# Seven of eight feed-forward layers read their tokens in another order, on one Trainium2 core

## The chip, the cores and the metric

The program runs on one core of one Trainium2 chip. The metric is the device time of one execution in microseconds, from the core's first instruction to its last with what lies around it. The median of the two timed runs of the kernel before is 2019.77 us, and both runs gave that same number.

## The reference: what is computed

An encoder of 4 blocks works on 256 tokens of width 1024. Each block adds to the residual stream a half-weighted SwiGLU feed-forward layer, then a mixer, then another half-weighted feed-forward layer; each part starts with an RMS norm. The mixers are a gated short convolution (blocks 0 and 3), a Hyena long convolution (block 1) and a gated delta rule (block 2). A last RMS norm ends it. The part that matters here is the feed-forward layer, eight times:

```
def swiglu(x, w_in, w_out):            # D = 1024, D_FF = 2816
    g, u = jnp.split(x @ w_in, 2, axis=-1)
    return (jax.nn.silu(g) * u) @ w_out

x = x + 0.5 * swiglu(rms_norm(x, norms[i, 0]), ffn_w_in[i, 0], ffn_w_out[i, 0])
```

All numbers are float32, and each product is computed to nearly that precision.

## The kernel before, in words

**Layout.** Activations are held transposed: features on the 128 partitions, the 256 tokens along each partition. A tile of the residual stream `x` is 128 x 512, two blocks of 128 features side by side, each with 256 tokens.

**Products.** Every operand of a large product is split into a high and a low part of type float32r (`wh`, `wl` for the weights; `xh`, `xl` for the normed input; `hh`, `hl` for the gated hidden values). The helper `mm3` (lines 325 to 329) then issues three matmuls into the same PSUM area: high times high (L327), low weight times high (L328), high weight times low (L329). In each, a 128 x 128 block of weights is the stationary operand, loaded by its own weight-load instruction, and 128 x 256 of tokens is the moving operand that streams through, one column for each token. The product is accumulated into 256 float32 columns of PSUM, half a bank.

**A feed-forward layer** (`ffn`, line 465). For each of 22 blocks of 128 hidden features, `proj` (line 302) forms gate and up parts over the 8 blocks of input features, into the two halves of the PSUM tile `g`: 2 x 8 calls of `mm3`. VectorE and ScalarE scale, apply SiLU, multiply and split the result (`gate`, line 471, and `split`, line 452). Two blocks later `acc_pair` (line 400) multiplies that hidden block by its row block of `w_out` into eight output areas, the halves of the four PSUM tiles `accf`: 8 calls of `mm3`. So a layer has 22 x 24 x 3 = 1584 matmuls and as many weight loads. Near the start of each layer a few small matmuls in plain float32 sum the squares (`pst`, L373) and spread the norm factor (`pbc`, L383). `finish` (line 412) adds the four accumulators to `x` and prepares the next layer's operands tile by tile.

**The order of the work.** The order of each engine's instructions is that in which the program text issues them. Weights come in 1 MB transfers on SyncE's queue into a ring of 2 buffers, ScalarE (L282) and VectorE (L284) split them into rings of 5 buffers, and TensorE uses one pair for 24 matmuls. Waits between engines come from the tiles' readers and writers. In layer 0 the preparation of the Hyena filters runs between the products, among it three-matmul products with 512 columns (`sp`).

**Numbering.** The 12 parts are numbered 0 to 11 (`norm_index`): feed-forward layers are 0, 2, 3, 5, 6, 8, 9 and 11; the mixers are 1 (short convolution), 4 (Hyena), 7 (delta rule) and 10 (short convolution). `run` (line 1483) goes through them.

Of the kernel before, what the change touches and what calls it, by code (L numbers as in the profile page):

```python
# [20 lines left out]
L = 256  # L21
# [25 lines left out]
def norm_index(ph):  # L47
    if ph[0] == "ffn":
        return ph[1] * 3 + 2 * ph[2]
    return ph[1] * 3 + 1  # L50
# [70 lines left out]
class Cols:  # L121
    def __init__(self):
        self.n = 0
        self.at = {}
# [90 lines left out]

class Prog:
    def __init__(self, nc, tc, io, phases, pools):
        self.nc, self.tc, self.io, self.phases = nc, tc, io, phases  # L220
# [103 lines left out]

    def mm3(self, out, ah, al, bh, bl, start, stop):
        mm = self.nc.tensor.matmul
        mm(out, ah, bh, start=start, stop=False, skip_group_check=True)  # L327
        mm(out, al, bh, start=False, stop=False, skip_group_check=True)  # L328
        mm(out, ah, bl, start=False, stop=stop, skip_group_check=True)  # L329
# [1153 lines left out]
    def run(self):  # L1483
        tc = self.tc
        self.setup()
        self.start()
        ph = self.phases
        ng = norm_index(ph[0])
        self.split_x(0, ng)
        self.ready.append(self.cut_part())  # L1490
        for m in range(1, 4):
            self.split_x(m, ng)
        self.ready.append(self.cut_part())
        self.ready.append(self.cut_part())
        for m in range(4):
            self.square_x(m, ng)
        kinds = [p[0] for p in ph]
        hyp = fip = None
        if "hy" in kinds:
            hyp = tc.tile_pool(name="hp", bufs=1)  # L1500
            self.hp = hyp.__enter__()
            fip = tc.tile_pool(name="fp", bufs=1)
            self.fp = fip.__enter__()
            self.hy_setup()
        self.setup_rest()
        for n, p in enumerate(ph):
            nxt = norm_index(ph[n + 1]) if n + 1 < len(ph) else None
            ng = norm_index(p)
            if nxt is None:
                tqp = tc.tile_pool(name="tq", bufs=1)  # L1510
                self.tq = tqp.__enter__()
                self.final_setup()
            if p[0] == "ffn":
                self.ffn(ng, nxt)
            elif p[0] == "sc":
                self.sc(ng, p[2], nxt)
            elif p[0] == "hy":
                self.drain_bg()
                fip.__exit__(None, None, None)
                with tc.tile_pool(name="tq", bufs=1) as self.tq:  # L1520
                    self.hy(ng, nxt)
                hyp.__exit__(None, None, None)
            else:
                with tc.tile_pool(name="gq", bufs=1) as self.gq:
                    self.gd(ng, nxt)
        self.final()
        tqp.__exit__(None, None, None)
# [49 lines left out]
```

## Time and profile before

| What | Value |
|---|---|
| Median of two runs | 2019.77 us (both the same) |
| The profiled execution's own time | 2015.31 us |
| Its span, first to last instruction | 2013.4 us |
| Mean granted TensorE clock | 0.993 |
| Matmuls, and weight loads | 17234 each |
| TensorE matmul busy (modelled ends) | 99% of the span |
| VectorE, ScalarE busy | 70%, 50% |
| HBM traffic | 353.11 MB read, 176 GB/s |

How to read it: PE is TensorE's matmul side and PEld its weight-load side, which overlap. Matmuls are pipelined, so the duration printed for one matmul is longer than the time from its start to the next one's start. It is that second number, the pace, that adds up to the span; it comes from counting matmuls in a stretch or from the starts in the timeline.

### The profile page before, as it was taken

The numbers are of one execution on the slowest core, as the hardware profiler recorded it, in microseconds if no ns is written. First come the engines' busy times: TensorE is split into PE (matmuls) and PEld (weight loads), VectorE is DVE, ScalarE is ACT, GpSimd is POOL, SyncE is SP. The second block draws the span as 40 slices with busy tenths as digits, with TensorE's granted clock in tenths as the row PEclk, the third lists the DMA queues.
The fourth block names the chain that finished last, engine by engine and source line by source line (L and its number), as shares of the span: only waits on it lengthen the run. The fifth ranks groups of instructions, "written<-read, shape, count | busy, mean of one in ns | idle before, by whom it ended". The sixth has DMA issues, their size and how long they took to land.

```text
span 2013.4 us, 40294 instructions
## 1 busy us (share of the span) xinstructions
PE 1986.9 (99%) x17234; PEld 1966.1 (98%) x17234; DVE 1405.1 (70%) x2155; ACT 1015.0 (50%) x1546; POOL 74.0 (4%) x75
## 2 busy tenths in 40 slices
PE   9999999999999999999999999899999999999998
PEld 9999999999999999999999988789999999999998
DVE  6765867666766798666766689957667666777664
ACT  6444545445544555444544467545445544545443
POOL 0000000000000120000000012000000000000000
PEclk9999999999999999999999999899999999999999
DMA  7644445555555533555555633304654655565552
GB/s 246 233 167 167 168 168 186 184 184 180 196 201 191 178 142 123 208 188 189 184 193 191 208 126 126 127 23 174 205 197 167 218 192 191 186 209 176 201 193 101
DMA packets 93989, 356.76 MB, mean 177 GB/s; under 512 B 5809, under 2 KB 7217, under 8 KB 93618
## 3 DMA queue, kind: packets, MB, share of 16 engines
q1 hardware_dynamic: 93666, 354.18, 50.7%
q8 instruction: 135, 2.21, 0.4%
q14 instruction: 44, 0.36, 0.1%
q10 hardware_dynamic: 144, 0.00, 0.0%
HBM read 353.11 MB, written 1.05 MB: 176 GB/s over the span
## 4 chain that ended last, share of the span: by engine, by line
PE 87%; DVE 7%; DMA 2%; ACT 2%; issue 1%; POOL 0%; SPq 0%; POOLq 0%; DVEq 0%; ACTq 0%
PE g L329 16%; PE g L328 16%; PE g L327 16%; PE accf L329 8%; PE accf L328 8%; PE accf L327 8%; DVE wl L284 2%; DMA raw<-w 2%; PE c L328 1%; PE c L327 1%; PE c L329 1%; PE accs L328 1%; PE b L328 1%; PE accs L327 1%; PE b L327 1%
## 5 line engine op out<-in xcount | busy, mean ns | idle before, releaser
L284 DVE TENSOR_TENSOR wl<-raw,wh 128x1024 fp32r<-128x1024 f32 (+1 forms) x667 | 810.8, 1221 | 396.6 <-ACT wh L282 396.1
L282 ACT ACTIVATE wh<-raw 128x1024 fp32r<-128x1024 f32 (+1 forms) x667 | 695.8, 1052 | 604.9 <-PE g L329 401.9
L327 PE MATMUL g<-xh,wh 128*128 128x256 f32 x2816 | 783.7, 278 | 0.1
L329 PE MATMUL g<-xl,wh 128*128 128x256 f32 x2816 | 782.4, 278 | 0.0
L328 PE MATMUL g<-xh,wl 128*128 128x256 f32 x2816 | 782.2, 278 | 0.1
L327 PEld LDWEIGHTS g<-xh,wh 128*128 128x128 f32 x2816 | 529.3, 188 | 3.1 <-ACT wh L282 2.7
L328 PEld LDWEIGHTS g<-xh,wl 128*128 128x128 f32 x2816 | 529.8, 188 | 0.5 <-DVE wl L284 0.4
L329 PEld LDWEIGHTS g<-xl,wh 128*128 128x128 f32 x2816 | 529.2, 188 | 0.0
L329 PE MATMUL accf<-hl,wh 128*128 128x256 f32 x1408 | 390.8, 278 | 0.8 <-DVE hl L458 0.8
L327 PE MATMUL accf<-hh,wh 128*128 128x256 f32 x1408 | 390.4, 277 | 0.0
L328 PE MATMUL accf<-hh,wl 128*128 128x256 f32 x1408 | 390.4, 277 | 0.0
L327 PEld LDWEIGHTS accf<-hh,wh 128*128 128x128 f32 x1408 | 264.1, 188 | 1.2 <-ACT hh L457 0.8
L329 PEld LDWEIGHTS accf<-hl,wh 128*128 128x128 f32 x1408 | 264.2, 188 | 1.0 <-DVE hl L458 1.0
L328 PEld LDWEIGHTS accf<-hh,wl 128*128 128x128 f32 x1408 | 264.4, 188 | 0.1
L457 ACT ACTIVATE hh<-t 128x256 fp32r<-128x256 f32 x192 | 79.7, 415 | 195.3 <-DVE t L477 189.3
L458 DVE TENSOR_TENSOR hl<-t,hh 128x256 fp32r<-128x256 f32 x192 | 81.3, 424 | 69.6 <-ACT hh L457 69.6
L474 DVE TENSOR_TENSOR t<-g,rs 128x256 f32<-128x256 f32 x176 | 74.4, 423 | 63.5 <-PE g L329 56.9
L475 ACT ACTIVATE t<-t 128x256 f32<-128x256 f32 x176 | 71.0, 404 | 27.0 <-DVE t L474 26.8
L328 PE MATMUL p<-xh,wl 128*128 128x256 f32 x256 | 73.5, 288 | 8.8 <-DVE wl L284 8.8
L327 PE MATMUL p<-xh,wh 128*128 128x256 f32 x256 | 74.8, 292 | 2.0 <-ACT wh L282 2.0
L477 DVE TENSOR_TENSOR t<-t,t 128x256 f32<-128x256 f32 x176 | 73.6, 418 | 1.6 <-ACT t L475 1.4
L329 PE MATMUL p<-xl,wh 128*128 128x256 f32 x256 | 73.2, 286 | 0.0
(315 smaller groups left out, 2407.0 us busy)
## 6 DMA issues: line engine op xcount, KB each, us to landing
raw<-w SPq DMA_DIRECT2D x330, 1024.0 KB, 4.7
raw<-w SPq DMA_DIRECT2D x6, 256.0 KB, 5.4
x<-x SPq DMA_DIRECT2D x4, 256.0 KB, 4.4
raw<-w SPq DMA_DIRECT2D x2, 512.0 KB, 6.3
dec<-dec SPq DMA_DIRECT2D x1, 1024.0 KB, 7.2
traw<-dft SPq DMA_DIRECT2D x2, 512.0 KB, 6.3
out<-ob SPq DMA_DIRECT2D x4, 256.0 KB, 2.4
w<-w SPq DMA_DIRECT2D x1, 512.0 KB, 9.1
```

The source lines that it names most:

```text
L282: nc.scalar.activation(hi[:, s], src[:, s], AF.Copy)
L284: nc.vector.tensor_tensor(lo[:, s], src[:, s], hi[:, s].bitcast(F32), op=ALU.subtract)
L327: mm(out, ah, bh, start=start, stop=False, skip_group_check=True)
L328: mm(out, al, bh, start=False, stop=False, skip_group_check=True)
L329: mm(out, ah, bl, start=False, stop=stop, skip_group_check=True)
L457: self.nc.scalar.activation(hh, src, AF.Copy)
L458: self.nc.vector.tensor_tensor(hl, src, hh.bitcast(F32), op=ALU.subtract)
L474: nc.vector.tensor_tensor(t1, pg[f][:, :L], self.rs, op=ALU.mult)
L475: nc.scalar.activation(t1, t1, AF.Silu)
L477: nc.vector.tensor_tensor(t2, t1, t2, op=ALU.mult)
```

## The change

A table gives seven of the eight feed-forward layers an order for the 256 tokens, and `mm3` applies it to the two moving operands and to the output area alike, where the moving operand has 256 columns. The k-th column that streams in is another token than before, and its result goes to that token's place in PSUM, so that PSUM holds the same values at the same places. The stationary operands, the number of matmuls, all other engines' instructions and all transfers are as before. Layer 11 and the mixers have no entry and keep the plain order.

```
+ORDERS = {
+    0: ("p (a b c) -> p b a c", 2, 16),
+    2: ("p (b a c) -> p a b c", 2, 16),
+    3: ("p (b a c) -> p a b c", 4, 16),
+    5: ("p (a b c) -> p b a c", 2, 8),
+    6: ("p (a b c) -> p b a c", 2, 4),
+    8: ("p (a b c) -> p b a c", 4, 16),
+    9: ("p (a b c) -> p b a c", 2, 32),
+}
+
+def ordered(ap, ng):
+    if ng not in ORDERS:
+        return ap
+    how, a, c = ORDERS[ng]
+    return ap.rearrange(how, a=a, c=c)
...
     def mm3(self, out, ah, al, bh, bl, start, stop):
         mm = self.nc.tensor.matmul
+        if bh.shape[1] == L:
+            out, bh, bl = (ordered(t, self.layer) for t in (out, bh, bl))
         mm(out, ah, bh, start=start, stop=False, skip_group_check=True)
         mm(out, al, bh, start=False, stop=False, skip_group_check=True)
         mm(out, ah, bl, start=False, stop=stop, skip_group_check=True)
...
-            ng = norm_index(p)
+            self.layer = ng = norm_index(p)
```

In words, with the tokens cut into runs of c neighbours (a float32 has 4 bytes):

| Layer | Order of the runs | Run | Runs in 256 |
|---|---|---|---|
| 0 | one of the first half, one of the second half, in turn | 16 tokens, 64 bytes | 16 |
| 2 | all even-numbered runs, then all odd-numbered | 16, 64 bytes | 16 |
| 3 | every fourth run, in four passes | 16, 64 bytes | 16 |
| 5 | first half, second half, in turn | 8, 32 bytes | 32 |
| 6 | first half, second half, in turn | 4, 16 bytes | 64 |
| 8 | the four quarters in turn | 16, 64 bytes | 16 |
| 9 | first half, second half, in turn | 32, 128 bytes | 8 |

## Rows read from the trace of the kernel before

**Rows 1.** The profile page: its head line and TensorE's busy time.

```profile
span 2013.4 us, 40294 instructions
...
PE 1986.9 (99%) x17234; PEld 1966.1 (98%) x17234; DVE 1405.1 (70%) x2155; ACT 1015.0 (50%) x1546; POOL 74.0 (4%) x75
```

**Rows 2.** The page's chain of work that ended last, shares by engine.

```profile
PE 87%; DVE 7%; DMA 2%; ACT 2%; issue 1%; POOL 0%; SPq 0%; POOLq 0%; DVEq 0%; ACTq 0%
```

**Rows 3.** Groups by shape on TensorE: count, busy us, mean ns, idle before.

```profile
L327 PE MATMUL g<-xh,wh 128*128 128x256 f32 x2816 | 783.7, 278 | 0.1
...
L327 PE MATMUL accf<-hh,wh 128*128 128x256 f32 x1408 | 390.4, 277 | 0.0
```

**Rows 4.** Waits of TensorE, the longest in total: us, times, longest.

```profile
PE p L328 <- DVE wl L284: 8.8, 2, 5.8
```

**Rows 5.** Stretches of layers 2, 3, 5, 6, 8, 9, 11, 0: length; busy and count by engine.

```profile
330.00:490.00 160.00, 160.00 (x1361) 160.00 (x1360) 98.59 (x135) 71.63 (x95) 0.00 (x0) 1.00 0.56 191
520.00:680.00 160.00, 160.00 (x1414) 160.00 (x1413) 102.82 (x141) 76.07 (x103) 0.00 (x0) 1.00 0.58 197
810.00:980.00 170.00, 170.00 (x1446) 170.00 (x1445) 106.90 (x146) 77.70 (x103) 0.00 (x0) 1.00 0.53 187
1000.00:1160.00 160.00, 160.00 (x1414) 160.00 (x1414) 102.27 (x141) 74.43 (x99) 0.00 (x0) 1.00 0.58 198
1390.00:1550.00 160.00, 160.00 (x1414) 160.00 (x1414) 105.44 (x146) 76.58 (x103) 0.00 (x0) 1.00 0.60 205
1570.00:1730.00 160.00, 160.00 (x1414) 160.00 (x1413) 103.48 (x143) 75.92 (x102) 0.00 (x0) 1.00 0.59 203
1840.00:1990.00 150.00, 150.00 (x1326) 150.00 (x1326) 97.02 (x131) 71.03 (x94) 0.00 (x0) 1.00 0.56 194
...
72.00:112.00 40.00, 40.00 (x342) 40.00 (x341) 27.26 (x41) 20.07 (x26) 0.00 (x0) 1.00 0.65 218
```

**Rows 6.** Timeline of layer 3 around `pbc`: start us, duration us, instruction.

```profile
509.32 0.28 PE L328 MATMUL g<-xh,wl 128*128 128x256 f32 x1
...
510.15 0.28 PE L329 MATMUL g<-xl,wh 128*128 128x256 f32 x1
510.27 0.38 PE L383 MATMUL pbc<-msk,r 128*128 128x128 f32 x2
...
510.60 0.28 PE L328 MATMUL g<-xh,wl 128*128 128x256 f32 x1
...
511.51 0.28 PE L327 MATMUL g<-xh,wh 128*128 128x256 f32 x1
```

**Rows 7.** Timeline of layer 2 at its `pbc`.

```profile
322.99 0.43 PE L383 MATMUL pbc<-msk,r 128*128 128x128 f32 x2 [0.24 <-POOL r L377]
...
323.38 0.28 PE L328 MATMUL g<-xh,wl 128*128 128x256 f32 x1
...
323.73 0.28 PE L328 MATMUL g<-xh,wl 128*128 128x256 f32 x1
```

**Rows 8.** Timeline of layer 0: twelve float32r matmuls of 512 columns.

```profile
168.03 0.39 PE L327 MATMUL sp<-eoh,th 128*128 128x512 f32 x1
...
169.64 0.39 PE L328 MATMUL sp<-eoh,tl 128*128 128x512 f32 x1
...
170.55 0.40 PE L329 MATMUL sp<-eol,th 128*128 128x512 f32 x1
```

**Rows 9.** Timeline of layer 7: eight weight loads for narrow matmuls, then 512-column matmuls.

```profile
1183.85 0.98 PEld L927 LDWEIGHTS ew<-g,msk 128*128 128x128 f32 x8
...
1184.74 0.30 PEld L916 LDWEIGHTS dc<-B,msk 128*128 128x128 f32 x2
...
1185.71 0.38 PE L917 MATMUL dc<-outside,idb 128*128 128x512 bf16 x1
1185.93 1.02 PE L916 MATMUL dc<-B,msk 128*128 128x512 f32 x2
1186.79 0.38 PE L917 MATMUL dc<-outside,idb 128*128 128x512 bf16 x1
```

## The prediction, made before the change was run

> **What bounds the kernel now.** I read the page's head first [rows 1]: 17234 matmuls in 2013.4 us, 117 ns for each on average, and TensorE busy 99% of the time. Then the chain of waits [rows 2]: 87% of it is TensorE's own work, so the reader sees an engine that follows itself. Then the groups by shape [rows 3]: the three lines of `mm3` in `g` (3 x 2816) and in `accf` (3 x 1408) are 12672 matmuls, 1584 in each of eight layers, with next to no idle time before them. The longest sum of TensorE's waits is 8.8 us, and it is in a mixer [rows 4]. So the end is set by the pace of the 256-column matmuls, and the printed 278 ns says nothing on that; counts in a stretch do.
>
> **Two paces.** The stretches inside the layers [rows 5], length by count: layers 2 and 5 give 160/1361 and 170/1446, both 117.6 ns; layers 3, 6, 8, 9 and 11 give 160/1414 and 150/1326, 113.1 or 113.2 ns; layer 0 about 117 (40/342). The granted clock is 1.00 in all of them, so this is not the clock. Same instructions, same shapes, two paces, each kept for a whole layer. Layer 3 shows where the pace is chosen [rows 6]: 7 steps take 0.83 us before the `pbc` pair (118.6 ns), 8 steps take 0.91 us after it (113.8 ns). In layer 2 the same pair waits for the norm factor, and the three steps behind it take 0.35 us (117 ns) [rows 7]. A layer on the slower pace costs 1584 x 4.4 ns = 7.0 us. The profiled execution took 2015.31 us, 4.46 us under the median of 2019.77; that is two thirds of one such layer, so I take it as about the size by which one execution differs from another here.
>
> **What sets the pace.** A column needs 0.417 ns at the 2.4 GHz level that is granted, 256 columns 106.7 ns. The 113.2 ns are 6% over that. A weight load is 128 columns: eight loads in a row start 0.89 us before the next, 111.3 ns each [rows 9], which could be the bound. But matmuls of 512 columns have two load times to hide one load in, and they too take 229 ns on average over 11 steps, 227.5 over the last four, where 213.3 would do [rows 8]: again 6 to 7% over. A bf16 matmul of 512 columns takes 0.22 us [rows 9]. So I read the pace as that at which float32r columns come through, in a stream without slack, with the loads close behind at 111.3 ns.
>
> **The change, part by part.** No instruction, load, wait or transfer is added, removed or moved. SyncE's queue, VectorE's readers of PSUM (which read the same area in the plain order) and the counts on all engines stay; VectorE, busy 99 us of 160 in a layer's stretch [rows 5], has room if TensorE should run faster. What changes is the address pattern of 7 x 1584 = 11088 matmuls, at the input and at the output. In place of one run of 256 columns there are 16, 16, 16, 32, 64, 16 and 8 runs (layers 0, 2, 3, 5, 6, 8, 9): 168 in all, 161 breaks, times 1584 are 255,024 breaks. The one question is the price of a break.
>
> The trace of before has no float32r matmul with a broken pattern. The nearest row is the bf16 matmul of 512 columns that reads one run of 128 four times, three breaks: 0.22 us to the next start, against 213.3 ns for its columns [rows 9]. At 215.5 ns (eight of them took 0.21 to 0.22) its excess is 2.2 ns, so a break costs at most 0.73 ns even if all of it is theirs: the upper end, 255,024 x 0.73 ns = 186 us, 2201 us. The lower end is a gain: if another order of the addresses takes away what holds the stream back, the loads hold it at 111.3 ns: 3 x 1584 x 6.3 + 4 x 1584 x 1.9 = 29.9 + 12.0 = 42 us, 1973 us. I take zero for a break, since the row with breaks is within 1% of its columns' bare time; then only the paces are drawn anew, each layer at one of its two. All three slow layers turned fast would give 4752 x 4.4 = 21 us back, all four fast ones turned slow cost 6336 x 4.4 = 28 us: 1994 to 2043.
>
> The Trainium skill, "TensorE: Matmul & The Clock Gate", section "Back-to-back issue gap", gives N/2.4 + 2.5 ns between matmuls, 109 ns for 256 columns. The trace does not agree, it has 113 and 118; by the page 4 to 8 ns in each matmul would be slack in which breaks could hide, and the first rival below would come to an estimated 2065 us rather than 2122.
>
> **The rivals.**
>
> First, slower: each break costs one column's time, 0.417 ns, in the stream that sets the pace. For it: the float32r stream already runs 16 columns' time late in 256 (113.2 - 106.7 = 6.5 ns), which the bf16 row does not, so something in that path pauses and new addresses may add pauses; nothing hides them. Against it: the bf16 row. Price 255,024 x 0.417 = 106 us: 2122. By layer, in ns for each matmul: 6 in layers 0, 2, 3, 8, 13 in layer 5, 26 in layer 6, 3 in layer 9. It passes 2% from 0.16 ns a break on. Chance 0.22, its size open between 2060 and 2201.
>
> Second, the pauses that exist come once in 16 columns, that is once in 64 bytes, and a run shorter than that brings its own. 6.5 ns are 16 pauses of one column's time, so the number fits, but nothing in the rows shows where in a matmul they fall. Then only layers 5 (16 more) and 6 (48 more) pay: 64 x 0.417 x 1584 = 42 us, 2057. Layer 6 alone would go from 113 to 133 ns. Chance 0.13, about half of it on either side of 2%.
>
> Third, PSUM takes the broken output at half pace. The row for that is the plain float32 matmul, which spends 0.86 us on 512 columns in two passes [rows 9], so 215 ns at 256 columns in two: 11088 x 100 ns = 1.1 ms, about 3100 us. No row speaks for it, none excludes it. Chance 0.04. The Trainium skill, "Advanced Engine Details and Errata", section "PSUM Cachelines", says that any non-contiguous pattern significantly slows matmuls, and next to it that every two consecutive elements should be contiguous; the shortest run here has four, so by its second sentence nothing happens. No run here shows either yet.
>
> Fourth, faster: the other orders free the stream down to the load's pace, 1973 us. For it: two paces under one instruction stream say that something interferes, and that it depends on how two streams meet. Against it: it would have to work in nearly all seven layers at once. Chance 0.05.
>
> Fifth, the change does nothing: the patterns of input and output are permuted alike, so a lowering that sorts them makes the plain order of both. Then 2015 to 2020. Chance 0.03.
>
> **How the numbers follow.** The forecast, breaks for nothing, has 0.53. I put it at 2017 us, between the profiled 2015.3 and the median 2019.8, since the paces may fall either way. 2% of the median is 40 us, about what a measurement of this kernel can tell from no change. Within 2%: 0.53 + 0.03 + 0.07 of the second rival = 0.63. Slower: 0.22 + 0.06 + 0.04 = 0.32. Faster: 0.05. The range begins at 1990, just under the forecast's own low end (the faster case left out, 0.05), and ends at 2125, just over the first rival's price (half of that rival, 0.11, and the third, 0.04, left out): 0.20 outside.
>
> **What would show it.** Pace by layer, from counts in the same stretches. Right: seven layers at 113 or 118, layer 6 no worse than layer 9, layer 11 as before. First rival: excess in proportion to the breaks, 7 : 15 : 31 : 63 for layers 9, 0, 5, 6. Second: layers 0, 2, 3, 8, 9 unchanged, 5 and 6 slower. Third: all seven near 215. Fourth: paces under 113. The mixers' paces may shift by the 4.4 ns with the layer ahead of them. The forecast is wrong if any layer leaves the two paces, above all layer 6 with its 64 runs.

## The result and the profile after

The changed kernel takes 2080.76 us (2079.63 and 2081.88), the kernel before 2019.77: slower by 3.0%, ratio 1.0302 with a 95% interval of 1.0258 to 1.0346. The profiled execution took 2079.63 us, 64.3 us over the profiled one of before. The time lies inside the range that was given, well above the 2017 us that was forecast.

The head of the page after, its chain of waits by engine, one matmul group and the longest wait of TensorE, to set against [rows 1 to 4]:

```profile
span 2077.9 us, 40314 instructions
...
PE 2053.6 (99%) x17234; PEld 2032.5 (98%) x17234; DVE 1406.8 (68%) x2155; ACT 1016.8 (49%) x1546; POOL 73.9 (4%) x75
...
PE 92%; DVE 4%; ACT 1%; DMA 1%; issue 1%; POOL 0%; SPq 0%; POOLq 0%; DVEq 0%; ACTq 0%
...
L349 PE MATMUL g<-xh,wh 128*128 128x256 f32 x2816 | 800.2, 284 | 0.3 <-ACT wh L302 0.3
```

```profile
PE p L350 <- DVE wl L304: 7.6, 2, 4.6
```

The counts of busy instructions on all five engines are the same (the 20 more in the head are of kinds not counted as busy), the longest wait is no longer than before, and TensorE's share of the chain has grown. So the time went into the pace. Stretches inside layers 2, 3, 5, 6, 8, 9, 11 and 0 of the kernel after (length; busy and count of PE, PEld, VectorE, ScalarE, GpSimd; clock, DMA share, GB/s), to set against [rows 5]:

```profile
330.00:490.00 160.00, 160.00 (x1336) 160.00 (x1335) 98.23 (x135) 71.34 (x95) 0.00 (x0) 1.00 0.54 185
520.00:680.00 160.00, 160.00 (x1350) 160.00 (x1349) 99.08 (x137) 72.26 (x96) 0.00 (x0) 1.00 0.53 185
830.00:990.00 160.00, 160.00 (x1299) 160.00 (x1299) 94.49 (x128) 68.39 (x91) 0.00 (x0) 1.00 0.52 181
1020.00:1190.00 170.00, 170.00 (x1344) 170.00 (x1344) 99.13 (x136) 74.24 (x97) 0.00 (x0) 1.00 0.50 175
1430.00:1590.00 160.00, 160.00 (x1350) 160.00 (x1349) 101.28 (x139) 73.61 (x100) 0.00 (x0) 1.00 0.56 191
1620.00:1780.00 160.00, 160.00 (x1336) 160.00 (x1335) 97.66 (x133) 71.10 (x94) 0.00 (x0) 1.00 0.54 190
1900.00:2050.00 150.00, 150.00 (x1326) 150.00 (x1326) 100.16 (x140) 73.16 (x98) 0.00 (x0) 1.00 0.57 197
72.00:112.00 40.00, 40.00 (x336) 40.00 (x335) 27.10 (x40) 19.49 (x26) 0.00 (x0) 1.00 0.61 217
```

The reader divides length by count. (A count takes in two or three matmuls that are under way at the ends of the stretch, so each pace is low by about 0.2 ns, by about 0.6 in layer 0's short stretch; the differences hardly change.) Each layer has 1584 of these matmuls.

| Layer | Runs | ns before | ns after | us added |
|---|---|---|---|---|
| 0 | 16 of 64 bytes | 117.0 | 119.0 | 3.3 |
| 2 | 16 of 64 bytes | 117.6 | 119.8 | 3.5 |
| 3 | 16 of 64 bytes | 113.2 | 118.5 | 8.5 |
| 5 | 32 of 32 bytes | 117.6 | 123.2 | 8.9 |
| 6 | 64 of 16 bytes | 113.2 | 126.5 | 21.1 |
| 8 | 16 of 64 bytes | 113.2 | 118.5 | 8.5 |
| 9 | 8 of 128 bytes | 113.2 | 119.8 | 10.5 |
| 11 | plain | 113.1 | 113.1 | 0 |

The last column adds up to 64.3 us. That the two profiled executions differ by the same 64.3 us is in part chance, for something else moved too: the mixer between layers 9 and 11, whose products are plain in both kernels, fell from the faster plain pace to the slower. A stretch of it before, then after:

```profile
1750.00:1810.00 60.00, 60.00 (x532) 60.00 (x531) 45.52 (x69) 29.75 (x37) 0.00 (x0) 1.00 0.61 207
```

```profile
1810.00:1870.00 60.00, 60.00 (x511) 60.00 (x511) 43.66 (x67) 28.42 (x36) 0.00 (x0) 1.00 0.60 207
```

That is 112.8 and 117.4 ns. From the last matmul of layer 9 to the first of layer 11 it took 87.9 us before and 91.2 after, 3.3 us more. Read in the same way, from starts in the traces, the seven layers took 62.2 us longer and the delta rule's part 1.1 us less. So about 62 of the 64 us are the price of the new order.

### The profile page after: what moved, and what is told of

The parts are those of the page before. It is cut to its first block, busy times and chain, and to the rows that moved or that the text cites. A ratio compares the mean times of both kernels' runs of the same rounds, so it can differ in the third digit from the quotient of the medians.

```text
span 2077.9 us, 40314 instructions
## 1 busy us (share of the span) xinstructions
PE 2053.6 (99%) x17234; PEld 2032.5 (98%) x17234; DVE 1406.8 (68%) x2155; ACT 1016.8 (49%) x1546; POOL 73.9 (4%) x75
## 4 chain that ended last, share of the span: by engine, by line
PE 92%; DVE 4%; ACT 1%; DMA 1%; issue 1%; POOL 0%; SPq 0%; POOLq 0%; DVEq 0%; ACTq 0%
PE g L349 16%; PE g L350 16%; PE g L351 16%; PE accf L349 8%; PE accf L351 8%; PE accf L350 8%; PE c L350 1%; PE c L351 1%; PE c L349 1%; DVE wl L304 1%; DMA raw<-w 1%; PE accs L350 1%; PE xv L351 1%; PE accs L351 1%; PE b L350 1%; PE b L351 1%
## 5 line engine op out<-in xcount | busy, mean ns | idle before, releaser
L349 PE MATMUL g<-xh,wh 128*128 128x256 f32 x2816 | 800.2, 284 | 0.3 <-ACT wh L302 0.3
L350 PE MATMUL g<-xh,wl 128*128 128x256 f32 x2816 | 798.7, 284 | 0.8 <-DVE wl L304 0.8
L351 PE MATMUL g<-xl,wh 128*128 128x256 f32 x2816 | 798.7, 284 | 0.0
L349 PE MATMUL accf<-hh,wh 128*128 128x256 f32 x1408 | 399.4, 284 | 0.0
L351 PE MATMUL accf<-hl,wh 128*128 128x256 f32 x1408 | 399.3, 284 | 0.0
L350 PE MATMUL accf<-hh,wl 128*128 128x256 f32 x1408 | 399.1, 283 | 0.0
```

## The experiments

Theories at the start: A, the read of the moving operand pays; B, the write into PSUM pays; C, the stream and the weight loads get in each other's way. Each is told apart by pace and not by total alone, because each layer can carry an order of its own. All rows are of the view just shown. Where no number of runs is given, a total is of one execution.

### Input or output

Only the moving operands are reordered in the first kernel, only the output in the second, so in both the products land on other tokens' places:

```
-            out, bh, bl = (ordered(t, self.layer) for t in (out, bh, bl))
+            bh, bl = (ordered(t, self.layer) for t in (bh, bl))     # in_only
+            out = ordered(out, self.layer)                          # out_only
```

> The new orders at the moving operand alone; the output goes to PSUM in the plain order, so the products of seven layers land on other tokens' places. Theory A, the read of the moving operand in SBUF is what pays: paces as with the whole change, 120 ns in layers 0, 2 and 9, 118.8 in 3 and 8, 123.4 in 5, 126.7 in 6, about 2080 us. Theory B, the write into PSUM pays: all layers at 113 or 118 ns, 2010 to 2030 us. Both pay: paces between, 2030 to 2065 us.

> The mirror image: the new orders at the output alone, the moving operand read in plain order (again the results land on other tokens' places). Theory A (read): 113 or 118 ns in every layer, 2010 to 2030 us. Theory B (write): the paces of the whole change, about 2080 us, with layer 6 at 127 ns.

The input alone took 2082.48 us, the output alone 2020.65, beside 2018.34 for the kernel before. Layers 6 and 9 of the input-only kernel, then layers 2, 6 and 11 of the output-only kernel:

```profile
1020.00:1190.00 170.00, 170.00 (x1345) 170.00 (x1344) 99.55 (x138) 74.58 (x98) 0.00 (x0) 1.00 0.52 177
...
1620.00:1780.00 160.00, 160.00 (x1336) 160.00 (x1335) 99.06 (x136) 71.62 (x96) 0.00 (x0) 1.00 0.55 188
```

```profile
330.00:490.00 160.00, 160.00 (x1361) 160.00 (x1360) 98.42 (x135) 71.74 (x95) 0.00 (x0) 1.00 0.56 191
...
1000.00:1150.00 150.00, 150.00 (x1325) 150.00 (x1325) 96.32 (x133) 70.48 (x94) 0.00 (x0) 1.00 0.58 198
...
1840.00:1990.00 150.00, 150.00 (x1276) 150.00 (x1275) 94.86 (x128) 69.65 (x92) 0.00 (x0) 1.00 0.56 194
```

126.4 and 119.8 ns with the input reordered, as in the whole change; 117.6 and 113.2 with the output reordered, as before. Theory A holds and B falls: the whole price is in the read. (Layer 11, untouched in both, is at 117.6 in the output-only kernel and was at 113.1 in [rows 5]; of that below.)

### Run length, and what a break costs

```
+    0: ("p (a b c) -> p b a c", 2, 64),
+    2: ("p (a b c) -> p b a c", 2, 8),
+    3: ("p (a b c) -> p b a c", 2, 16),
+    5: ("p (a b c) -> p b a c", 2, 4),
+    6: ("p (a b c) -> p b a c", 2, 32),
+    8: ("p (a b c) -> p b a c", 2, 2),
+    9: ("p (a b c) -> p b a c", 8, 16),
+    11: ("p (a b c) -> p b a c", 2, 64),
```

> The whole change with other entries, to part run length from layer: first half and second half in turn with runs of 64 columns in layer 0, 8 in layer 2, 16 in layer 3, 4 in layer 5, 32 in layer 6, 2 in layer 8, 64 in layer 11; layer 9 takes every second run of 16. Theory of a price for each break (the first rival of the prediction, resized): excess over 113 ns in proportion to the breaks, so layers 0 and 11 (4 runs) within 1 ns of 113 or 118 and layer 8 (128 runs) near 140 ns or more. Theory that two streams meet and lock into step: a few fixed paces that don't go with the number of breaks, 120 ns in layers 3 and 6 as it was in layers 0, 2 and 9, about 123.4 in layer 2, 126.7 in layer 5, whatever pace the layer had before.

It took 2161.21 us. Layers 0, 2, 3, 5, 6, 8, 9, 11:

```profile
72.00:112.00 40.00, 40.00 (x340) 40.00 (x341) 28.19 (x42) 20.12 (x28) 0.00 (x0) 1.00 0.68 230
330.00:490.00 160.00, 160.00 (x1299) 160.00 (x1299) 94.78 (x129) 68.98 (x92) 0.00 (x0) 1.00 0.53 181
530.00:690.00 160.00, 160.00 (x1335) 160.00 (x1335) 95.91 (x129) 70.59 (x92) 0.00 (x0) 1.00 0.53 185
830.00:990.00 160.00, 160.00 (x1265) 160.00 (x1264) 93.22 (x127) 70.59 (x92) 0.00 (x0) 1.00 0.51 173
1040.00:1200.00 160.00, 160.00 (x1350) 160.00 (x1350) 97.48 (x133) 70.84 (x95) 0.00 (x0) 1.00 0.55 188
1430.00:1660.00 230.00, 230.00 (x1355) 230.00 (x1354) 99.50 (x137) 74.73 (x96) 0.00 (x0) 1.00 0.39 133
1700.00:1860.00 160.00, 160.00 (x1336) 160.00 (x1335) 96.50 (x131) 71.58 (x94) 0.00 (x0) 1.00 0.54 186
1980.00:2130.00 150.00, 150.00 (x1276) 150.00 (x1276) 94.51 (x130) 69.80 (x92) 0.00 (x0) 1.00 0.57 195
```

Runs of 64 columns: 117.6 ns. 32: 118.5. 16: 119.9 and 119.8. 8: 123.2. 4: 126.5. 2: 169.7. A price for each break would make these rise in step with 3, 7, 15, 31, 63 and 127 breaks; instead 16 runs cost hardly more than 8, and from 64 to 128 runs the price jumps by 43 ns. The pace goes with the order and not with the layer: 16 columns give 120 in layer 3, which was a fast layer before, as they did in layers 0 and 2. It does not go with the length of the run alone: runs of 16 in four passes or from four quarters took 118.5 in the change, and runs of 32 took 118.5 here and 119.8 in layer 9 of the change. But for that last difference the second theory's list of paces held; that two streams lock into step, the reason it gave, is not shown by this.

Whether runs of 64 columns are free could not be read from that, as 117.6 is also the slower plain pace. So all seven layers got them:

```
+ORDERS = {n: ("p (a b c) -> p b a c", 2, 64) for n in (0, 2, 3, 5, 6, 8, 9)}
```

> The change with one order in all seven layers: first half and second half in turn, runs of 64 columns (256 bytes, 4 runs in a matmul). If such runs are free: layers 3, 6, 8 and 9 at 113.3 ns, 2 and 5 at 117.7, as in the kernel before, 2010 to 2025 us. If any break costs: all seven layers at 117.7 ns or more, 28 us over the kernel before, about 2045 us.

2018.8 us beside 2017.73 for the kernel before. Layers 3 and 6:

```profile
520.00:670.00 150.00, 150.00 (x1326) 150.00 (x1326) 96.02 (x131) 70.13 (x93) 0.00 (x0) 1.00 0.56 193
...
1000.00:1150.00 150.00, 150.00 (x1326) 150.00 (x1325) 95.55 (x130) 70.27 (x93) 0.00 (x0) 1.00 0.57 199
```

113.1 ns, as plain: runs of 256 bytes are free.

### The weight loads

```
+        half = bh.shape[1] == L and self.layer % 3 != 1
...
         mm(out, ah, bh, start=start, stop=False, skip_group_check=True)
+        if half:
+            out, ah, al = out[:64], ah[:, :64], al[:, :64]
```

> In every feed-forward layer the second and third matmul of each product load and use 64 of their 128 weight columns (the low-order terms of half the outputs are left out); tokens as many as before. Layers 0, 3, 8 and 11 in the plain order, 2 with runs of 16 from the two halves, 5 with 8, 6 with 4, 9 with 16 from the four quarters. Theory C, stream and weight loads get in each other's way: with a third of the load columns gone the mean pace falls towards 107 to 110 ns in plain layers, and the ordered layers lose at least a third of their excess over 107 (13, 17, 20 ns). Theory D, the stream pays by itself: paces as before, 113 or 118 plain, 120, 123.4, 126.7, 118.8 in the ordered ones.

2071.89 us. Layers 3 (plain), 5 (runs of 8), 6 (runs of 4) and 9 (four quarters in turn, runs of 16):

```profile
520.00:680.00 160.00, 160.00 (x1367) 160.00 (x1366) 98.55 (x134) 72.31 (x95) 0.00 (x0) 1.00 0.55 190
820.00:980.00 160.00, 160.00 (x1299) 160.00 (x1299) 94.68 (x129) 68.96 (x92) 0.00 (x0) 1.00 0.52 180
1020.00:1190.00 170.00, 170.00 (x1333) 170.00 (x1332) 95.77 (x130) 72.43 (x93) 0.00 (x0) 1.00 0.51 176
...
1620.00:1780.00 160.00, 160.00 (x1369) 160.00 (x1368) 100.01 (x136) 72.57 (x97) 0.00 (x0) 1.00 0.55 192
```

117.0, 123.2, 127.5 and 116.9 ns: with a third of the load columns gone no layer with runs of 8 or 4 is quicker, and the plain ones are not near 110. So theory C's forecast falls, and shorter loads do not take the price of a broken order away. Theory D does not hold to the letter either: plain layers 3, 8 and 11 all came to 117.0, neither of the two paces before, and the four quarters took 116.9 where the change had 118.5. So the edit, which halves the loads and the outputs of two matmuls in three, does shift the pace by a few ns; how is open.

### Wraps or addresses

A broken pattern does two things: its inner part begins anew for each run (a wrap), and the address jumps. Here the first run is streamed again and again, so it wraps as often but stays in place; the output is plain.

```
+REPEAT = {0: 64, 2: 8, 3: 16, 5: 4, 6: 32, 8: 2, 9: 128, 11: 16}
...
+    return ap[:, :c].unsqueeze(1).to_broadcast((P, L // c, c))
```

> The output plain; the moving operand of every feed-forward layer is its first run, streamed again and again until 256 columns are full (so the products are of the first tokens alone): runs of 64 columns in layer 0, 8 in 2, 16 in 3, 4 in 5, 32 in 6, 2 in 8, 128 in 9, 16 in 11. As many breaks as in the run-length experiment, but the addresses never leave one run. Theory W, the wrap of the pattern is what costs: 113 or 118 ns in layers 0 and 9, about 120 in 3, 6 and 11, 123 in 2, 127 in 5, 170 in 8. Theory J, the jump to a far address is what costs (512 bytes there, at most the run's own length here): short runs cost less than long ones, layers 2, 3, 5, 8 and 11 at 113 ns or under.

2037.86 us. Layers 2 (runs of 8), 3 (16), 5 (4), 6 (32), 8 (2) and 9 (128):

```profile
330.00:480.00 150.00, 150.00 (x1345) 150.00 (x1344) 97.31 (x132) 70.85 (x94) 0.00 (x0) 1.00 0.59 203
510.00:670.00 160.00, 160.00 (x1311) 160.00 (x1310) 94.32 (x128) 69.73 (x92) 0.00 (x0) 1.00 0.53 181
820.00:970.00 150.00, 150.00 (x1345) 150.00 (x1344) 97.74 (x133) 71.13 (x95) 0.00 (x0) 1.00 0.57 200
1000.00:1160.00 160.00, 160.00 (x1336) 160.00 (x1335) 95.17 (x129) 70.25 (x93) 0.00 (x0) 1.00 0.54 186
1390.00:1540.00 150.00, 150.00 (x1345) 150.00 (x1344) 102.10 (x143) 74.76 (x102) 0.00 (x0) 1.00 0.59 203
1580.00:1730.00 150.00, 150.00 (x1275) 150.00 (x1275) 93.11 (x127) 69.19 (x91) 0.00 (x0) 1.00 0.55 190
```

Runs of 8, 4 and 2 all give 111.5 ns, whether with 32, 64 or 128 runs in a matmul: a wrap by itself has no price that shows. A float32r stream that stays within 32 bytes is quicker than the plain one. Its pace is close to that of the weight loads in [rows 9] (111.3 ns, there for matmuls in plain float32); that the loads are then the bound fits, but no run tested it. Theory W falls. Theory J was right on short runs and misjudged runs of 16: going back 64 bytes after each 16 columns costs 122.0 ns, more than the jump of 512 bytes does (119.9). So the length of the jump is not the price either. What costs is an address that does not go straight on, unless it stays within 32 bytes; why the line lies between 32 and 64 bytes is open.

### Alignment

The moving tiles begin some columns into slightly longer allocations, so that runs start off a boundary (o is 2 columns, 8 bytes, in layers 0, 3, 5 and 6; 4 in layers 2, 8 and 11; 8 in layer 9). To fit, a pad of 80 columns ahead of them shrank to 48.

```
+        hh = pool.tile([P, L + 16], F32R, name=f"hh{name}", tag="hh", bufs=4)[:, o:o + L]
```

> The moving tiles begin some columns into their allocation, so that runs begin off a 64-byte or off a 16-byte boundary. Layers 3 and 11 plain, shifted by 2 and 4 columns; halves in turn with runs of 16: layer 0 shifted by 2, layer 2 by 4, layer 9 by 8; runs of 8 in layer 5 shifted by 2; runs of 4 in layer 6 shifted by 2, in layer 8 by 4. Theory S, the number of 16-byte pieces that a matmul touches sets the price (64 plain and for aligned runs of 4 or more, 128 at runs of 2, which took 170 ns): a shift by 4 or 8 changes nothing (120 in layers 2 and 9, 127 in 8), a shift by 2 makes 128 pieces in layer 6 (about 170), 96 in layer 5 (about 148), 80 in layer 0 (about 137), 65 in layer 3 (113 or 118). If boundaries of 64 bytes matter, layers 2 and 9 rise too. If only the breaks matter: 120, 123, 127 as unshifted.

2299.05 us. Layers 0, 2, 3, 5, 6, 8 and 9:

```profile
72.00:112.00 40.00, 40.00 (x268) 39.42 (x268) 23.84 (x39) 15.89 (x22) 0.00 (x0) 1.00 0.57 198
380.00:540.00 160.00, 160.00 (x1321) 160.00 (x1320) 94.88 (x128) 69.87 (x93) 0.00 (x0) 1.00 0.54 185
570.00:730.00 160.00, 160.00 (x1330) 160.00 (x1329) 96.25 (x133) 70.78 (x94) 0.00 (x0) 1.00 0.54 186
880.00:1120.00 240.00, 240.00 (x1373) 240.00 (x1372) 100.85 (x138) 74.69 (x97) 0.00 (x0) 1.00 0.37 127
1160.00:1390.00 230.00, 230.00 (x1367) 230.00 (x1366) 98.75 (x135) 73.35 (x95) 0.00 (x0) 1.00 0.38 133
1630.00:1800.00 170.00, 170.00 (x1347) 170.00 (x1347) 101.24 (x138) 74.71 (x98) 0.00 (x0) 1.00 0.52 180
1830.00:1990.00 160.00, 160.00 (x1329) 160.00 (x1328) 98.39 (x135) 70.77 (x95) 0.00 (x0) 1.00 0.55 189
```

A shift by 16 or 32 bytes does next to nothing (121.1, 126.2, 120.4 where unshifted runs took 119.9, 126.5, 119.9). A shift by 8 bytes takes runs of 16 from 119.0 (layer 0 of the change) to 149.3 ns, runs of 8 from 123.2 to 174.8 and runs of 4 from 126.5 to 168.3, and the plain stream of layer 3 from 113.2 to 120.3. So 16 bytes is a boundary that the read sees, and 64 bytes is none that shows. Theory S, the count of 16-byte pieces touched, gets the order of cost wrong: 96 pieces (174.8) cost more than 128 (168.3), and it was low for 80 pieces (137 expected, 149.3 measured) and for 65 (113 or 118, 120.3). The Trainium skill, "Advanced Engine Details and Errata", section "SBUF Cachelines", names 16-byte lines and asks for at least two accesses on a line. The trace agrees on the 16 bytes. But aligned runs of 4 or more float32r columns make at least four accesses on each line that they touch, which by that section is full performance, and in the change they paid 2 to 13 ns.

### Half the bytes in a column, and another type

High and low parts of weights and tokens become bf16 in the feed-forward layers, in the same tiles:

```
+        if i in self.short:
+            hi, lo = hi.bitcast(BF16)[:, :D], lo.bitcast(BF16)[:, :D]
```

> In the feed-forward layers the high and low parts are bf16 rather than float32r, in weights and tokens alike (so the products keep fewer bits); three products as before. Layers 0, 3, 11 plain; halves in turn with runs of 16 in layer 2, 8 in 5, 4 in 6, 2 in 8; four quarters in turn, runs of 16, in 9. If the price of a broken stream is one of the bytes that the read has to deliver (my reading of why the bf16 row misled me): all plain layers at 107 to 110 ns with no two paces, and the broken ones within 1 ns of them, save perhaps runs of 2. If a break has a price of its own: layers 2, 5, 6 lie 2 to 13 ns over the plain ones, as float32r did.

1992.74 us. Layers 2 (runs of 16), 3 (plain), 5 (runs of 8), 6 (4) and 8 (2):

```profile
320.00:460.00 140.00, 140.00 (x1285) 125.48 (x1284) 92.73 (x127) 68.37 (x91) 0.00 (x0) 1.00 0.60 204
490.00:630.00 140.00, 140.00 (x1285) 125.48 (x1283) 93.57 (x129) 68.12 (x90) 0.00 (x0) 1.00 0.59 204
780.00:930.00 150.00, 150.00 (x1377) 134.44 (x1375) 100.26 (x138) 73.87 (x98) 0.00 (x0) 1.00 0.59 204
960.00:1100.00 140.00, 140.00 (x1238) 117.35 (x1236) 89.59 (x121) 66.31 (x87) 0.00 (x0) 1.00 0.55 196
1350.00:1530.00 180.00, 180.00 (x1319) 128.97 (x1318) 94.91 (x128) 71.16 (x91) 0.00 (x0) 1.00 0.48 162
```

108.9 ns plain, 108.9 with runs of 16 and of 8, 113.1 with runs of 4 (8 bytes), 136.5 with runs of 2 (4 bytes). Runs of 16 and 8 columns, which cost float32r 2 to 6 ns, are free, and a price starts at shorter runs. This is what the bytes reading said, save that runs of 4 already pay 4 ns. But bytes and type changed together here: that the bytes are what counts is argued, and no run has one without the other. (The loads are shorter too in this kernel, but shorter loads alone made neither plain layers nor runs of 8 or 4 quick in the experiment on loads.) The Trainium skill, "TensorE: Matmul & The Clock Gate", section "Back-to-back issue gap", gives 109 ns at 256 columns for a single matmul by itself; the bf16 stream agrees with it, the float32r stream (113 and 118) does not.

### The two plain paces

```
+                if f == KICK and ng in (2, 5, 11):          # KICK = 4
+                    for z in range(2):
+                        nc.tensor.transpose(pg[f][:, z * P:(z + 1) * P], self.ident, self.ident)
```

> The kernel before, in the plain order, with two transposes of the identity put in ahead of the gate product of hidden block 4 in layers 2, 5 and 11 (their output is overwritten by that product). Theory: a layer's pace, 113.3 or 117.7 ns, is drawn whenever such a small matmul breaks the stream, and a pair that doesn't wait has left 113.3 behind it in 8 of 9 cases. Then layers 2 and 5 go to 113.3 and give back about 6.5 us each, less 0.3 us for each pair: about 2005 us where the kernel before takes 2018 to 2020. Rival: the pace belongs to the layer (its place in the rings, its data): layers 2 and 5 stay at 117.7, 2019 to 2021 us.

2019.97 us (12 runs), ratio 1.0009, interval 0.9994 to 1.0025: no change. The timeline of layer 2 behind the pair:

```profile
341.24 0.38 PE L490 MATMUL g<-msk 128*128 128x128 f32 x2
...
341.58 0.28 PE L329 MATMUL g<-xh,wl 128*128 128x256 f32 x1
...
342.29 0.28 PE L329 MATMUL g<-xh,wl 128*128 128x256 f32 x1
```

Layers 5 and 11 behind theirs:

```profile
825.00:970.00 145.00, 145.00 (x1234) 145.00 (x1233) 88.40 (x120) 64.56 (x85) 0.00 (x0) 1.00 0.55 188
1840.00:1990.00 150.00, 150.00 (x1276) 150.00 (x1275) 96.53 (x134) 70.26 (x96) 0.00 (x0) 1.00 0.56 195
```

Six steps in 0.71 us, 118 ns, and 117.5 and 117.6 in layers 5 and 11. My theory, that each small matmul draws the pace anew, falls with three misses in three. The rival got the time, but it is not right as stated either: layer 11 had 113.1 ns in [rows 5] and 117.6 here and in two other kernels that leave it plain (150/1276, with the output reordered and with runs of 64). What sets this pace is open.

### A quicker version, with fewer bits

The bf16 kernel with every layer in plain order:

> The bf16 experiment with the plain order in all eight feed-forward layers (fewer bits in the products than the kernel before). Each layer at 109.2 ns, like the plain layers there: layer 6 gives back 1584 x 4.2 = 6.6 us and layer 8 1584 x 27.5 = 43.6 us of the 1992.7 us measured there, so about 1942 us, 3.7% under the kernel before. Rival: ScalarE or VectorE, which cut the weights, can't keep up at the higher pace, and TensorE waits: 1955 us or more.

1946.79 us (4 runs), ratio 0.965 (0.9624 to 0.9677) to the kernel before. Layers 6 and 8:

```profile
960.00:1100.00 140.00, 140.00 (x1285) 125.49 (x1283) 93.16 (x128) 68.19 (x90) 0.00 (x0) 1.00 0.60 207
1340.00:1480.00 140.00, 140.00 (x1285) 125.48 (x1284) 95.11 (x132) 69.74 (x94) 0.00 (x0) 1.00 0.60 211
```

108.9 ns, as expected (the starts in the trace give 109.2), and a total 5 us over the sum: by starts in the two bf16 traces layers 6 and 8 gave back 49 of the 50 us, and the mixers, which the edit does not touch, took 4 us more. The rival's waits are not there. It is quicker than both kernels, but it keeps fewer bits in each product and so is no replacement at equal precision. No order of all 256 float32r columns that was tried beat the plain one.

## Why the prediction was wrong

**What bounds the kernel: right in the main.** TensorE's own pace set the end, and broken reads cost time at once, so the stream had no slack for them. "With the loads close behind at 111.3 ns" is likely, not shown: that row is of loads for matmuls in plain float32, and streams that stay in 32 bytes stopped near it, at 111.5. The reading that layer 3's small `pbc` matmuls show "where the pace is chosen" did not carry over: three pairs of small matmuls put into slow layers left the pace at 118.

**The price of a break: the step that failed.** "I take zero for a break, since the row with breaks is within 1% of its columns' bare time" took one price for every break from one row, and that row differs from the change in two ways that the runs show to matter. Its runs are of 128 bf16 columns, 256 bytes, while those of the change are of 128 to 16 bytes. At 256 bytes breaks are free in float32r as well (113.1 ns with runs of 64 columns), so the row could not show the price of a shorter run in any type. And it is bf16, in which runs of 32 and 16 bytes are free (108.9 against 108.9), while in float32r they cost 5.6 and 13.3 ns. The prediction had a warning in its own numbers: the same bf16 row had no 6% excess, the float32r rows had it. In place of zero the breaks cost 2.0 to 13.3 ns in each matmul, 62 to 64 us in all, and not one price for each break: it depends on the length of the run and on the order. Even the upper end, 0.73 ns a break, was passed in layer 9: 6.6 ns for 7 breaks are 0.94 ns each. What in the read makes it so stays open. ("Eight of them took 0.21 to 0.22" holds for seven; behind the eighth the next matmul starts 0.03 us later. The price it gave is hardly touched.)

**The first rival: right side, wrong law.** One column's time for each break gave 106 us and excesses of 7 : 15 : 31 : 63 in layers 9, 0, 5, 6. Measured over each layer's own pace before they are 6.6, 2.0, 5.6 and 13.3 ns. Its price for layer 6 was 26 ns and came out at half, for layer 9 it was 3 and came out at double.

**The second rival: wrong.** Runs of 64 bytes are not free (layers 0, 2, 3, 8), and a shift off the 64-byte boundary changed next to nothing (119.9 to 121.1 and 120.4).

**The third: wrong.** The output's order is free at runs of four and more. Of the two sentences in the section "PSUM Cachelines" of the Trainium skill's "Advanced Engine Details and Errata", the first (any non-contiguous pattern slows matmuls significantly) does not agree with the trace, 113.2 ns in layer 6 with the output alone reordered; the second (pairs should be contiguous) is not contradicted, but no run here splits a pair.

**The fourth and fifth: wrong.** No broken float32r order that reads all tokens came under the faster plain pace, and the change did reach the chip.

**The range** held the time by luck: its upper part comes from the first rival's 2122 us, whose law the runs refute, and not from the forecast, whose own low and high ends were 1994 and 2043. The chances did not favour the side either, 0.32 for slower.

## What to carry to other kernels

Before a price is taken from "the nearest row", ask in what that row differs from yours: here its runs were at least twice as long in bytes, which alone hides the price, and its type was another, which hides most of it. Where TensorE is busy 99%, divide the length of a stretch by its count, layer by layer; the total alone would have told neither the runs nor the two plain paces apart. Keep the moving operand of float32r matmuls in runs of 256 bytes or more that start on 16 bytes; reorder at the output, where it was free down to runs of 16 bytes.

## What was not expected of the hardware

- A float32r stream that repeats 8, 16 or 32 bytes runs at 111.5 ns, quicker than the contiguous one at 113 or 118; repeating 64 bytes makes it 122.0.
- A start 8 bytes off a 16-byte boundary costs runs of 8 columns 51.6 ns in each matmul (123.2 to 174.8), more than halving the run to 4 does (3.3).
- Seventeen executions of the unchanged kernel in one series ran from 2009.85 to 2023.16 us. Two paces 4.4 ns apart, 7.0 us for each layer, would give such a spread, though no trace shows it for the seventeen; what chooses between them, and why 8 runs cost as much as 16, these runs don't say.
